# A two-layer encoder trunk: cosine product out of PSUM, first convolution steps on ScalarE, a pad of 32 bytes

## The chip, the cores and the metric

The kernel runs on one core of one Trainium2 chip. The metric is the device time of one execution in microseconds (us). The engines are TensorE (PE, matmuls into PSUM), VectorE (DVE), ScalarE (ACT), GpSimd (POOL) and SyncE (SP), whose queue here issues most DMA transfers. Each engine works through its own list of instructions in order; semaphores tie the lists together. PEclk in the profile is the granted clock of TensorE as a share of 2.4 GHz; 0.50 is 1.2 GHz.

## What is computed

Two sequences (1024 and 512 tokens, width 1024, fp32) go through two layers with shared weights and a last norm. Cut to the parts that the change and its neighbours touch:

```python
def apply_rope(x, cos, sin):                 # q and k of both attentions
    x1, x2 = jnp.split(x, 2, axis=-1)
    rot = jnp.concatenate([-x2, x1], axis=-1)
    return x * cos + rot * sin

def even_layer(h, ...):                      # layer 0
    u = h @ w_in
    glu, a_gate, q, k, v, b_gate = split_cols(u, EVEN_SPLITS)
    a_val, a_glu = jnp.split(glu, 2, axis=-1)
    a = a_val * jax.nn.sigmoid(a_glu)
    a = layernorm(depthwise_conv(a, conv_w, conv_b), ln_g, ln_b)      # 31 taps
    a = jax.nn.silu(a) * jax.nn.silu(a_gate)
    o = windowed_gqa(apply_rope(q), apply_rope(k), v, sink) * jax.nn.silu(b_gate)
    return jnp.concatenate([a, o], axis=-1) @ w_out

def odd_layer(h, ...):                       # layer 1
    q, k, v, c_gate, z, xbc, dt_f, dt_b = split_cols(h @ w_in, ODD_SPLITS)
    c = diff_attention(apply_rope(q), apply_rope(k), v, lam, diff_g) * jax.nn.silu(c_gate)
    xbc = jax.nn.silu(depthwise_conv(xbc, conv_w, conv_b))            # 5 taps
    d = mamba2_bidir(z, xbc, dt_f, dt_b, ...)                         # two chunked scans
    return jnp.concatenate([c, d], axis=-1) @ w_out
# x = x + layer(rmsnorm(x)) twice, then rmsnorm
```

## The kernel before

The 1536 tokens are three chunks of 512 (`g` = 0, 1 of the long sequence, 2 of the short one), channels lie on the 128 partitions. A projection tile is 128 output channels by 512 tokens: `proj` (L280 to L282) makes 24 matmuls of 128x512 into one PSUM accumulator, three for each of eight input blocks, since every fp32 operand is split into a high and a low half. The high half of a weight is a ScalarE copy (`wh`, L268), the low one a GpSimd subtraction (`wl`, L269).

The program runs in phases. A1: input norm, and of layer 0 the GLU projections, the 31-tap convolution (four units of 128 channels, each over all three chunks), the rotary k and q, some gates, and `conv_ln`, the layer norm over the convolved channels. A2: windowed attention and output projection. B1a: layer 1's dt and `xbc` projections with the 5-tap convolution, eight tiles of 128 channels. B1z: z and v. B1b: the scans, with layer 1's rotary k and q between them. B2: differential attention and output. O1: the last projection and norm.

What the change touches:

- `rope` (L374 to L385), 15 calls in A1 and 24 in B1b. ScalarE copies the accumulator into `r` (L378), four DMAs fetch the swapped halves into `rs` (L381), VectorE multiplies `r` by the cosines in place (L382), GpSimd multiplies `rs` by the sines (L383), VectorE adds (L384), a DMA writes the result. `r` and `rs` are two of four buffers of the tag `e2`, which the gates (L371, L372) and the tanh of the GLU (L428) share.
- `conv_units` (L433 to L471). When the three GLU products of a unit (L430, VectorE, one for each chunk, reading the value accumulator in PSUM) are there, `begin` sums neighbours into `xs` (L440) and starts three partial filters `fir` (L444, L446, L447); `taps` adds 15, 14 and 15 more products to them (L453, L456, L458), all in place on VectorE, 768 elements a partition each. `end` joins them (L464 to L466), and from the second unit on adds the unit to a sum (L471).
- `conv_ln` (L473 on): a mean matmul for each chunk (L479) into the tag `msx`, which has one bank in A1, four subtractions (L482) and squares, and then the scaling (L490, L491).
- `xbc` (L704 on): copies into `a` (L709), a first step on VectorE (L713), four taps (L716), Silu (L718).
- The PSUM accumulators of A1 rotate over five banks (`pj` and four `pjx`); in B1b nearly all use the one `pj`.

The order inside each engine's list is set when the program is built, by the framework's scheduler, which simulates a timeline and picks instructions that are ready; the source only gives priorities, by `merge` and `spread`, which lay projection units between convolution, scan and attention units. So an edit in one place can move instructions elsewhere.

## Time and profile before

| | us |
|---|---|
| median of three runs | 1711.17 (1710.85 to 1715.9) |
| profiled execution | 1710.5 |
| its span | 1708.7 |
| TensorE busy | 1586.7 (93%) |
| VectorE busy | 1132.5 (66%) |
| ScalarE busy | 708.1 (41%) |
| GpSimd busy | 677.5 (40%) |
| mean granted clock | 0.979 |

TensorE is busy nearly all the time, so the time follows its idle moments and its clock. They are found by stage: the table of stretches gives busy time and clock, the waits say what ended each idle moment, the groups by line give the duration of one instruction, and a timeline shows one place in order. A busy share of VectorE says little alone: what counts is where TensorE waits for it.

### The profile page before, as it was taken

What the parts mean: (1) busy time and instruction counts of PE and PEld (TensorE: products, weight loads), DVE (VectorE), ACT (ScalarE), POOL (GpSimd) and SP (SyncE); (2) the same over time, 40 slices, a digit from 0 to 9 for tenths busy, and PEclk for the clock granted to TensorE, in tenths of its full rate; (3) what the DMA queues carried; (4) which work ended last, traced back from release to release, by engine and by line L of the source; (5) the groups of instructions that cost most, each with busy time, mean ns of one, the idle gap of its engine ahead of it and who ended that gap; (6) DMA issues with size and microseconds to landing.
All of it is one profiled execution on the core that took longest, in us unless ns stands there. A gap on an engine that the chain in (4) does not pass through costs nothing.

```text
span 1708.7 us, 22696 instructions
## 1 busy us (share of the span) xinstructions
PE 1586.7 (93%) x7868; PEld 1303.6 (76%) x7868; DVE 1132.5 (66%) x1631; ACT 708.1 (41%) x1440; POOL 677.5 (40%) x531
## 2 busy tenths in 40 slices
PE   4998998889988989999999999989998999999997
PEld 3776787668777867867788887778877877888887
DVE  6788999954788786646664003796635677678554
ACT  6210111144676664433433112222225767668542
POOL 4244333333656545631311004654444534442340
PEclk9999999989999999999999999999999999999999
DMA  9011023335455447731433216664553545442562
GB/s 371 29 53 47 32 74 98 113 104 175 126 169 184 150 145 232 236 111 37 131 105 130 78 50 189 198 180 141 158 150 124 149 131 147 138 133 75 178 198 99
DMA packets 159109, 229.45 MB, mean 134 GB/s; under 512 B 18279, under 2 KB 70567, under 8 KB 158994
## 3 DMA queue, kind: packets, MB, share of 16 engines
q1 hardware_dynamic: 157074, 227.40, 42.2%
q8 instruction: 62, 1.02, 0.3%
q0 software_dynamic: 1920, 0.59, 0.2%
q14 instruction: 53, 0.43, 0.1%
HBM read 153.15 MB, written 64.55 MB: 127 GB/s over the span
## 4 chain that ended last, share of the span: by engine, by line
PE 30%; DMA 7%; DVE 4%; issue 4%; POOL 2%; SPq 2%; ACT 2%; POOLq 0%; DVEq 0%; ACTq 0%
PE ms L992 3%; PE pj L280 3%; PE pj L281 3%; PE pj L282 3%; DMA e<-e 2%; PE pjx L747 2%; PE pjx L746 2%; PE pjx L748 2%; PE s L967 2%; PE s L968 2%; PE pjx L280 1%; PE pjx L281 1%; PE pjx L282 1%; POOL e L383 1%; PE tr L390 1%
## 5 line engine op out<-in xcount | busy, mean ns | idle before, releaser
L269 POOL TENSOR_TENSOR wl<-wr,wh 128x512 fp32r<-128x512 f32 (+1 forms) x169 | 274.0, 1625 | 366.0 <-ACT wh L268 325.7
L282 PE MATMUL pjx<-x,wl 128*128 128x512 f32 (+1 forms) x712 | 286.4, 404 | 19.9 <-POOL wl L269 19.9
L280 PE MATMUL pjx<-x,wh 128*128 128x512 f32 (+1 forms) x712 | 287.4, 404 | 12.5 <-DVE e L372 8.0
L281 PE MATMUL pjx<-x,wh 128*128 128x512 f32 (+1 forms) x712 | 287.9, 405 | 6.3 <-DVE x L202 5.0
L280 PE MATMUL pj<-x,wh 128*128 128x512 f32 x604 | 247.4, 410 | 9.3 <-DVE e L372 5.0
L281 PE MATMUL pj<-x,wh 128*128 128x512 f32 x604 | 244.3, 404 | 3.9 <-DVE x L202 3.9
L282 PE MATMUL pj<-x,wl 128*128 128x512 f32 x604 | 241.9, 400 | 0.0
L268 ACT ACTIVATE wh<-wr 128x512 fp32r<-128x512 f32 (+1 forms) x169 | 105.5, 625 | 205.9 <-PE pjx L281 86.5
L282 PEld LDWEIGHTS pjx<-x,wl 128*128 128x128 f32 (+1 forms) x712 | 135.2, 190 | 55.5 <-POOL wl L269 23.0
L280 PEld LDWEIGHTS pjx<-x,wh 128*128 128x128 f32 (+1 forms) x712 | 134.8, 189 | 49.6 <-DVE e L372 10.4
L281 PEld LDWEIGHTS pjx<-x,wh 128*128 128x128 f32 (+1 forms) x712 | 134.8, 189 | 41.4 <-DVE x L202 6.6
L280 PEld LDWEIGHTS pj<-x,wh 128*128 128x128 f32 x604 | 115.6, 191 | 36.0 <-DVE e L372 6.1
L281 PEld LDWEIGHTS pj<-x,wh 128*128 128x128 f32 x604 | 115.3, 191 | 30.2 <-DVE x L202 5.1
L282 PEld LDWEIGHTS pj<-x,wl 128*128 128x128 f32 x604 | 115.3, 191 | 26.5 <-issue 0.2
L383 POOL TENSOR_TENSOR e<-e,cs 128x512 f32<-128x512 f32 x39 | 64.8, 1660 | 106.5 <-DMA e<-e 96.9
L976 ACT ACTIVATE pr<-s,nmx 128x1024 f32<-128x1024 f32 (+1 forms) x96 | 93.3, 975 | 27.6 <-DVE nmx L970 15.7
L177 POOL TENSOR_TENSOR r<-v,mhalf 128x4 f32<-128x4 f32 (+2 forms) x37 | 33.0, 892 | 140.5 <-DVE v L173 91.6
L992 PE MATMUL ms<-v,pT 128*128 128x128 f32 x640 | 81.2, 278 | 6.5 <-ACT pT L989 4.0
L992 PEld LDWEIGHTS ms<-v,pT 128*128 128x128 f32 x640 | 77.9, 193 | 10.6 <-ACT pT L989 4.4
L970 DVE TENSOR_REDUCE nmx<-s 128x1 f32<-128x1024 f32 x64 | 76.8, 1217 | 10.1 <-PE s L968 9.7
L517 POOL TENSOR_TENSOR raw<-raw,q 128x1024 fp32r<-128x1024 f32 x24 | 58.2, 2425 | 53.4 <-ACT q L515 49.0
L569 POOL TENSOR_SCALAR pr<-pr,den 128x384 f32<-128x384 f32 (+1 forms) x96 | 55.4, 597 | 50.0 <-DVE den L567 26.2
(360 smaller groups left out, 3393.1 us busy)
## 6 DMA issues: line engine op xcount, KB each, us to landing
wr<-in_wo SPq DMA_DIRECT2D x96, 256.0 KB, 3.7
wr<-in_w SPq DMA_DIRECT2D x87, 256.0 KB, 3.0
e<-e SPq DMA_DIRECT2D x156, 64.0 KB, 2.0
x<-xbd SPq DMA_DIRECT2D x22, 384.0 KB, 3.9
ct<-x1d SPq DMA_DIRECT2D x29, 256.0 KB, 3.6
raw<-q0d SPq DMA_DIRECT2D x48, 128.0 KB, 3.0
ct<-cat0d SPq DMA_DIRECT2D x24, 256.0 KB, 3.1
x1d<-e SPq DMA_DIRECT2D x24, 256.0 KB, 3.1
```

Of the source, the lines that this page charges most:

```text
L268: S.activation(out=wh, in_=raw, func=AF.Copy)
L269: G.tensor_tensor(out=wl, in0=raw, in1=wh.bitcast(F32), op=ALU.subtract)
L280: T_.matmul(acc, wh[:, kk, :], xh[:, k, :], start=(k == ks[0]), stop=False)
L281: T_.matmul(acc, wh[:, kk, :], xl[:, k, :], start=False, stop=False)
L282: T_.matmul(acc, wl[:, kk, :], xh[:, k, :], start=False, stop=(k == ks[-1]))
L383: G.tensor_tensor(out=rs, in0=rs, in1=cs_["sin"][:, cs], op=ALU.mult)
L517: G.tensor_tensor(out=lo, in0=raw, in1=q.bitcast(F32), op=ALU.subtract)
L569: G.tensor_scalar(out=prs[j], in0=prs[j], scalar1=den[:, j:j + 1], scalar2=1.0, op0=ALU.mult, op1=ALU.mult)
L746: T_.matmul(acc, xh[:, k, ts], hi[k], start=(k == 0), stop=False)
L970: V.tensor_reduce(out=nmx[:, t:t + 1], in_=o, axis=AX.XY, op=ALU.max, negate=True)
L976: S.activation(out=pr, in_=o if ncs > 1 else o[:, u:u + 1, :], func=AF.Exp, bias=nmx[:, u:u + 1], accum_out=den[:, u:u + 1])
L992: T_.matmul(oacc, pT[:, i, :], vtok[:, kt, :], start=(kt == 0), stop=(kt == NB - 1))
```

## The change

The cosine product of a rope is taken from the PSUM accumulator by VectorE, in a scalar_tensor_tensor into a third buffer `o`, and no longer from `r` after the copy; `r` is only read by the shuffles. The first step of each of the three partial filters, and that of `xbc`, is a ScalarE activation with scale and bias in place of VectorE's tensor_scalar: 12 and 8 instructions. The tag `e2` gets two further buffers in A1 and B1b (`e2x`), so that a rope takes three of six. A tile of 8 floats that nothing reads is allocated ahead of the others and set to zero. Lines move by 6 or 7: L382 becomes L386, L384 L391, L430 L437, L453 L459, L456 L462, L458 L464, L479 L485.

```diff
-    "A1": (dict(cs=2, a=2, xs=1, fir=3, y6=5), dict(pjx=4, msx=1)),
+    "A1": (dict(e2x=2, cs=2, a=2, xs=1, fir=3, y6=5), dict(pjx=4, msx=1)),
...
-    "B1b": (dict(rk=2, lk=4, cs=2, p4=4, x3=2, bc=2, ...
+    "B1b": (dict(e2x=2, rk=2, lk=4, cs=2, p4=4, x3=2, bc=2, ...
...
     def sb(tag, shape, dt=F32):
+        extra = ph["sb"].get(tag + "x", 0)
+        if extra:
+            n = ph["sb", tag] = (ph.get(("sb", tag), -1) + 1) % (SHARED[tag] + extra)
+            if n >= SHARED[tag]:
+                tag += "x"
         if tag in SHARED:
...
+    V.memset(tiny(8, "pad", 1), 0.0)
...
     def rope(acc, scale, g, dst):
         cs = pos(g)
-        r, rs = sb("e2", (P, CH)), sb("e2", (P, CH))
+        r, rs, o = (sb("e2", (P, CH)) for _ in range(3))
         S.activation(out=r, in_=acc, func=AF.Copy, scale=scale)
+        V.scalar_tensor_tensor(out=o, in0=acc, scalar=scale, in1=cs_["cos"][:, cs], op0=ALU.mult, op1=ALU.mult)
         for b in range(4):
-            o = b ^ 1
-            dma(out=rs[32 * b:32 * b + 32, :], in_=r[32 * o:32 * o + 32, :])
-        V.tensor_tensor(out=r, in0=r, in1=cs_["cos"][:, cs], op=ALU.mult)
+            f = b ^ 1
+            dma(out=rs[32 * b:32 * b + 32, :], in_=r[32 * f:32 * f + 32, :])
         G.tensor_tensor(out=rs, in0=rs, in1=cs_["sin"][:, cs], op=ALU.mult)
-        V.tensor_tensor(out=r, in0=r, in1=rs, op=ALU.add)
-        dma(out=dst[:, tok(g)], in_=r)
+        V.tensor_tensor(out=o, in0=o, in1=rs, op=ALU.add)
+        dma(out=dst[:, tok(g)], in_=o)
...
-            V.tensor_scalar(out=f[0], in0=a[:, :, 1:512:2], scalar1=cwh[:, j, 0:1],
-                            scalar2=prm[:, PC_CB + j:PC_CB + j + 1], op0=ALU.mult, op1=ALU.add)
-            V.tensor_scalar(out=f[1], in0=a[:, :, 0:513:2], scalar1=cwh[:, j, 1:2], scalar2=None, op0=ALU.mult)
-            V.tensor_scalar(out=f[2], in0=xs[:, :, 0:256], scalar1=cws[:, j, 0:1], scalar2=cb2[:, j:j + 1],
-                            op0=ALU.mult, op1=ALU.add)
+            S.activation(out=f[0], in_=a[:, :, 1:512:2], func=AF.Identity, scale=cwh[:, j, 0:1],
+                         bias=prm[:, PC_CB + j:PC_CB + j + 1])
+            S.activation(out=f[1], in_=a[:, :, 0:513:2], func=AF.Copy, scale=cwh[:, j, 1:2])
+            S.activation(out=f[2], in_=xs[:, :, 0:256], func=AF.Identity, scale=cws[:, j, 0:1], bias=cb2[:, j:j + 1])
...
-        V.tensor_scalar(out=acc, in0=a[:, :, 0:CH], scalar1=prm[:, wc:wc + 1],
-                        scalar2=prm[:, PC_SB + j:PC_SB + j + 1], op0=ALU.mult, op1=ALU.add)
+        S.activation(out=acc, in_=a[:, :, 0:CH], func=AF.Identity, scale=prm[:, wc:wc + 1],
+                     bias=prm[:, PC_SB + j:PC_SB + j + 1])
```

VectorE at the start of conv unit 0, before: the last GLU product (L430) of the unit, the neighbour sum (L440), the three first steps and the first taps (L345 and L346 belong to a constant).

```order
L430 SCALAR_TENSOR_TENSOR a_342<-e_58_453,pj_480 128x512
L345 TENSOR_TENSOR nlam<-ls 128x1
L440 TENSOR_TENSOR xs_594<-a_342 128x813
L346 TENSOR_SCALAR nlam<-nlam 128x1
L444 TENSOR_SCALAR fir_596<-a_342,cwh,prm 128x768
L446 TENSOR_SCALAR fir_597<-a_342,cwh 128x771
L447 TENSOR_SCALAR fir_598<-xs_594,cws,cb_318 128x768
L453 SCALAR_TENSOR_TENSOR fir_596<-a_342,cwh,fir_596 128x768
L456 SCALAR_TENSOR_TENSOR fir_597<-a_342,cwh,fir_597 128x771
L458 SCALAR_TENSOR_TENSOR fir_598<-xs_594,cws,fir_598 128x768
```

The same place after the change:

```order
L437 SCALAR_TENSOR_TENSOR a_347<-e_59_458,pj_485 128x512
L352 TENSOR_TENSOR nlam<-ls 128x1
L447 TENSOR_TENSOR xs_599<-a_347 128x813
L353 TENSOR_SCALAR nlam<-nlam 128x1
L459 SCALAR_TENSOR_TENSOR fir_601<-a_347,cwh,fir_601 128x768
L462 SCALAR_TENSOR_TENSOR fir_602<-a_347,cwh,fir_602 128x771
L459 SCALAR_TENSOR_TENSOR fir_601<-a_347,cwh,fir_601 128x768
L464 SCALAR_TENSOR_TENSOR fir_603<-xs_599,cws,fir_603 128x768
L462 SCALAR_TENSOR_TENSOR fir_602<-a_347,cwh,fir_602 128x771
L459 SCALAR_TENSOR_TENSOR fir_601<-a_347,cwh,fir_601 128x768
```

The three first steps are gone from VectorE's list, and taps follow the neighbour sum at once.

TensorE at `conv_ln`, before: the mean matmuls of the first two chunks (L479) stand in the last block of the gate accumulator `pjx_2404`, three matmuls apart.

```order
L280 MATMUL pjx_2404<-x_30_195,wh_2399 128x512
L479 MATMUL msx_2027<-y_150_1239,mean_w 128x512
L281 MATMUL pjx_2404<-x_31_196,wh_2399 128x512
L282 MATMUL pjx_2404<-x_30_195,wl_2400 128x512
L479 MATMUL msx_2065<-y_150_1239,mean_w 128x512
L280 MATMUL pjx_2487<-x_46_280,wh_2393 128x512
```

After the change the first stands in `pjx_2334`, an accumulator that ran two earlier, the second (below the dots, which leave out 29 rows) in the accumulator behind it:

```order
L288 MATMUL pjx_2334<-x_48_286,wh_2265 128x512
L289 MATMUL pjx_2334<-x_47_285,wl_2266 128x512
L485 MATMUL msx_2047<-y_154_1247,mean_w 128x512
L287 MATMUL pjx_2334<-x_47_285,wh_2265 128x512
...
L287 MATMUL pj_2454<-x_37_237,wh_2420 128x512
L485 MATMUL msx_2085<-y_154_1247,mean_w 128x512
L288 MATMUL pj_2454<-x_38_238,wh_2420 128x512
```

Counted from the start of the list, the first mean matmul moved from row 1205 to row 1141, and the three are 32 and 29 rows apart where they were 3 and 35.

VectorE in B1b, one rope among scan operations, before: its cosine product (L382) and its add (L384) follow each other.

```order
L865 TENSOR_TENSOR p_1741_9713<-p_1741_9713,p_1743_9722 128x1024
L890 TENSOR_TENSOR t_9746<-ms_9743,ed 128x512
L870 TENSOR_TENSOR p_1741_9713<-p_1741_9713,tr_9725 128x1024
L382 TENSOR_TENSOR e_1733_9655<-e_1733_9655,cs_8391 128x512
L384 TENSOR_TENSOR e_1733_9655<-e_1733_9655,e_1734_9656 128x512
L876 TENSOR_TENSOR y_9729<-y_9729,msx_9731 128x512
```

After the change a rope's product (L386) reads the accumulator `pj`, and two scan operations stand between it and its add (L391); the next rope's product follows.

```order
L386 SCALAR_TENSOR_TENSOR e2x_9528<-pj_9501,cs_8415 128x512
L871 TENSOR_TENSOR p_1730_9549<-p_1730_9549,p_1732_9558 128x1024
L876 TENSOR_TENSOR p_1730_9549<-p_1730_9549,tr_9561 128x1024
L391 TENSOR_TENSOR e2x_9528<-e2x_9528,e2x_9527 128x512
L386 SCALAR_TENSOR_TENSOR e_1753_9644<-pj_9617,cs_8415 128x512
L882 TENSOR_TENSOR y_9565<-y_9565,msx_9567 128x512
```

The product now stands where its accumulator is complete, ahead of the shuffles' end, and the add stays behind the sine product.

## Rows read from the trace of the kernel before

**Rows 1.** The page, first part: busy time, share of the span, instructions by engine.

```profile
PE 1586.7 (93%) x7868; PEld 1303.6 (76%) x7868; DVE 1132.5 (66%) x1631; ACT 708.1 (41%) x1440; POOL 677.5 (40%) x531
```

**Rows 2.** By stage: stretch, length, busy us (count) by engine, PEclk, DMA share, GB/s.

```profile
285.00:360.00 75.00, 59.48 (x234) 44.63 (x233) 66.39 (x71) 16.01 (x28) 21.72 (x14) 0.93 0.32 102
360.00:680.00 320.00, 294.11 (x1470) 241.37 (x1469) 228.70 (x474) 191.25 (x441) 168.64 (x171) 0.98 0.53 165
680.00:840.00 160.00, 159.04 (x725) 122.40 (x725) 97.93 (x137) 65.78 (x102) 64.22 (x44) 0.99 0.43 131
...
1030.00:1290.00 260.00, 244.68 (x1184) 200.97 (x1183) 163.19 (x199) 67.64 (x107) 135.10 (x129) 0.99 0.57 170
1290.00:1610.00 320.00, 303.74 (x1807) 261.63 (x1805) 226.48 (x338) 225.53 (x519) 126.98 (x81) 0.98 0.41 125
```

**Rows 3.** TensorE's waits, 285 to 360 us: us in total, times, longest us.

```profile
PE pjx L280 <- DVE e L372: 8.0, 3, 4.2
PE pjx L280 <- ACT wh L268: 2.2, 1, 2.2
PE msx L479 <- DVE y L482: 2.1, 1, 2.1
PE pjx L282 <- POOL wl L269: 2.1, 1, 2.1
PE pj L280 <- DVE e L372: 1.2, 1, 1.2
```

**Rows 4.** TensorE's waits, 66 to 200 us; timelines (start, us) of GpSimd and VectorE.

```profile
PE pjx L282 <- POOL wl L269: 13.8, 3, 6.4
...
166.18 1.29 POOL L269 TENSOR_TENSOR wl<-wr,wh 128x512 fp32r<-128x512 f32 x1 [7.76 <-ACT wh L268]
180.61 11.28 POOL L269 TENSOR_TENSOR wl<-wr,wh 128x512 fp32r<-128x512 f32 x2 [13.14 <-ACT wh L268]
...
185.04 1.01 DVE L458 SCALAR_TENSOR_TENSOR fir<-xs,cws,fir 128x768 f32<-128x768 f32 x1
...
217.52 0.69 DVE L430 SCALAR_TENSOR_TENSOR a<-e,pj 128x512 f32<-128x512 f32 x1 [6.23 <-PE pj L282]
```

**Rows 5.** By stage, columns as in group 2: the stretch at half clock.

```profile
347.90:358.10 10.20, 5.86 (x11) 3.55 (x12) 4.35 (x8) 5.37 (x9) 2.37 (x1) 0.50 0.32 103
```

**Rows 6.** VectorE by line, 224.1 to 345.5 us: count, busy us, mean ns, idle before.

```profile
L456 DVE SCALAR_TENSOR_TENSOR fir<-a,cwh,fir 128x771 f32<-128x771 f32 x22 | 27.9, 1267 | 0.0
...
L382 DVE TENSOR_TENSOR e<-e,cs 128x512 f32<-128x512 f32 x12 | 13.2, 1098 | 0.3 <-DMA e<-e 0.3
...
L372 DVE SCALAR_TENSOR_TENSOR e<-e,pjx 128x512 f32<-128x512 f32 x5 | 3.4, 673 | 0.0
...
L444 DVE TENSOR_SCALAR fir<-a,cwh,prm 128x768 f32<-128x768 f32 x1 | 1.1, 1068 | 0.0
```

**Rows 7.** ScalarE's waits, 224 to 346 us.

```profile
ACT e L378 <- DVE e L384: 38.1, 7, 10.1
```

**Rows 8.** Timelines: VectorE's sum for conv_ln, then TensorE at conv_ln.

```profile
341.03 1.76 DVE L471 TENSOR_TENSOR y<-y,y 128x1536 f32<-128x1536 f32 x1
...
339.19 0.50 PE L280 MATMUL pjx<-x,wh 128*128 128x512 f32 x1 [0.96 <-DVE e L372]
...
344.19 0.39 PE L280 MATMUL pjx<-x,wh 128*128 128x512 f32 x1
344.42 1.02 PE L479 MATMUL msx<-y,mean_w 128*128 128x512 f32 x2
```

**Rows 9.** ScalarE by line, whole span: columns as in group 6.

```profile
L718 ACT ACTIVATE y<-y 128x1536 f32<-128x1536 f32 x8 | 11.9, 1488 | 21.3 <-DVE y L716 21.3
```

**Rows 10.** VectorE's waits, 1030 to 1290 us; timeline of one rope there.

```profile
DVE e L382 <- DMA e<-e: 38.4, 16, 5.8
...
1183.03 0.58 ACT L378 ACTIVATE e<-pj 128x512 f32<-128x512 f32 x1
...
1185.32 0.47 PE L280 MATMUL pj<-x,wh 128*128 128x512 f32 x1
```

2 lines of the change are left out of this document (1 added, 1 removed).

## The prediction

> **What bounds the kernel now.** I read the page's first part first: TensorE is busy for 1586.7 of 1708.7 us, so all that any change can win is its 122 us of idle time and what a halved clock costs [rows 1]. The table by stage says where that lies. What the reader is to see in [rows 2]: from 680 to 840 us TensorE idles for 1 us only, so nothing can be won there; the stretch 285 to 360 us has 15.5 us of idle time and a mean granted clock of 0.93, with VectorE busy for 66.4 of 75 us. There VectorE is the bound. The waits of TensorE in that stretch name it [rows 3]: 8.0 + 1.2 us for gate products (L372) that stand in VectorE's queue between convolution taps, 2.1 us for conv_ln's subtraction, and 4.3 us for weights whose ScalarE copy or GpSimd half came late. From 347.9 to 358.1 us the granted clock is 0.50, the 1.2 GHz level, right after these idle moments; 10.2 us at half speed lose 5.1 us [rows 5]. So about 15.6 + 5.1 = 20.7 us is the most that the stretch can give.
>
> Earlier in A1 (66 to 200 us) TensorE waits three times, 13.8 us in all, for the low half of a weight from GpSimd [rows 4]. Here two GpSimd subtractions in a row, with their inputs there, last 11.28 us together, while a single one lasts 1.29 us, and VectorE runs taps of 1.01 us without a gap, of which one row stands. GpSimd is held up for as long as that run of taps lasts.
>
> **The change part by part.** The profiled execution took 1710.5 us (span 1708.7, 1.8 outside it), 0.7 us below the median of 1711.17; I sum against 1710.5.
>
> *Conv steps, units 0 to 2.* Each unit's three first steps (1.07 us each, [rows 6]) leave VectorE. But the order of VectorE shows three more taps in their place before the next GLU product, which waits for TensorE anyway (6.23 us in the last of these waits, [rows 4]): 25, 33 and 36 taps stood there before, 28, 36 and 40 now. VectorE is given the same amount of work in front of the same wait, so the first two stalls for GpSimd stay: 0. At the third (beside the 11.28 us) the new ScalarE steps start only behind a tanh that ScalarE makes for the gate, so VectorE may have a gap in which GpSimd is let in. That can win between 0 and a third of the 13.8 us, 4.6; I take 2, nearer to nothing, since at the other two the taps close up.
>
> *From the last GLU product to conv_ln (224 to 343 us), VectorE.* Three things go. The first steps of unit 3: 3 x 1.07 = 3.2 us. Nine taps that are done earlier now (69 stood behind the last GLU product, 60 now): 9 x 1.27 = 11.4 us at the mean of this window [rows 6], 9 x 1.01 = 9.1 us at that of an undisturbed tap [rows 4]. And 12 cosine products of 1.098 us become products with an input in PSUM; the nearest row is L372, the same operation and shape out of PSUM, 0.673 us [rows 6]: 12 x 0.425 = 5.1 us, or 0, if a product that took long because GpSimd worked beside it only passes that on to a tap. The bounds are so 3.2 + 9.1 = 12.3 and 3.2 + 11.4 + 5.1 = 19.7 us; I take 15, the lower half, since GpSimd's products stay. VectorE ended this work at 341.03 + 1.76 = 342.8 us [rows 8]; now at about 328.
>
> *The same stretch, TensorE.* conv_ln's first mean matmul started at 344.4 us [rows 8]; in the new order it stands 64 matmuls further forward (the second fence of the section on the change), which at 0.23 us from start to start is 14.7 us. Before, TensorE passed that point at 344.4 - 14.7 - 2.2 = 327.5 us (2.2 us are the two gate waits in between, 1.2 and 0.96). Without the waits in front of it (2.2 + 2.1 for weights and 9.2 - 4.2 - 2.2 = 2.8 for a gate) it would be there at 320.4. But it can't pass before VectorE's 328: 0.5 us later than before, after a wait of some 7 us. What it lost behind that point was 2.2 + 2.1 + 4.2 us of waits and 5.1 us of clock, 13.6 us in all [rows 3, 5]. The three mean matmuls are some 30 matmuls (7 us) apart now instead of 3 matmuls, so the wait for their single bank should go, and the gate products should be done early, since VectorE is ahead. After the new wait of 7 us the clock may fall again as it did at 347.9 us. Gain 13.6 - 0.5 = 13.1 without a fall, 8.0 with all of it; with VectorE's 12.3 (2.7 us later) and a fall 5, with 19.7 and none 17.8. I take 10.
>
> *ScalarE in A1.* Its rope copies wait for the buffers that VectorE's add frees: 38.1 us over seven copies, up to 10.1, and weight copies queue behind them [rows 7]. Three buffers of six in place of two of four keep two ropes in flight as before; but the add comes sooner, since the product no longer waits for the shuffle. This is where the 2.2 + 2.1 us for weights in [rows 3] should go; they stand ahead of conv_ln's point and only bring TensorE to the wait there sooner, so I count nothing more. Twelve conv steps of 768 elements are added to ScalarE, between 0.58 us (512 elements, [rows 10]) and 1.49 us (1536, [rows 9]), about 1 us each, on an engine that is busy for 16 of 75 us [rows 2]: 0.
>
> *xbc steps (B1a).* Eight steps of 1536 elements leave VectorE, and eight of some 1.5 us (L718's, of the same shape) go to ScalarE [rows 9], with one more load of a function table (ten where nine stood). TensorE idles for 1 us of 160 there [rows 2], and ScalarE is busy for 66: nothing to win, up to 2 to lose where the copy that frees an accumulator queues behind a step; 0.5.
>
> What VectorE's steps are worth can be weighed otherwise. The row gives 1.07 us for 768 elements [rows 6], no faster than a tap. The Trainium skill ("VectorE: DVE Perf Modes", the perf-mode tier table) lets an fp32 tensor-scalar operation on SBUF operands run at two elements a cycle. By it the three steps of unit 3 would be worth about half, and the sum some 1.5 us less; the trace does not show that form in these steps, and the measured durations decide.
>
> *Ropes in B1b.* VectorE's 38.4 us of waiting for the shuffles move from the product to the add, where they are paid as well [rows 10]; TensorE does not see them. The new price is the bank: nearly all of these accumulators use one bank, which is free again only when the ScalarE copy and then the product have read it. In the shown rope the copy runs from 1183.03 to 1183.61 and the next accumulator starts at 1185.32, 1.7 us later [rows 10]. The product adds 0.67 us (L372's duration), and what VectorE has in hand at that moment, of the order of 1 us. That fits in the 1.7 us mostly. VectorE saves up to 24 x 0.425 = 10 us; if TensorE's 15.3 us of idle time [rows 2] shrink by a fifth, the gain is 3, and by a fifth of rival 2's price the loss is 5; taken +0.5.
>
> *A2, B2 and the pad.* No operation changes there, but the order does: gate matmuls that fill waits stand elsewhere. TensorE idles for 25.9 us in A2 and 16.3 us in B2 [rows 2]; a fifth of that either way is 5 us, taken 0. The pad moves later tiles by 32 bytes and adds one memset of 8 columns: operations on tiles at either offset last alike (0.673 us for L372, 0.69 for L430, [rows 4, 6]), so 0.
>
> Sum: -2 - 10 + 0.5 + 0.5 = -11; 1710.5 - 11 = 1699.5, against the median 1700.
>
> **Rivals.** *(1) The gain is eaten at conv_ln.* TensorE arrives early at the mean matmul that was put forward, waits the full 7 us, and its clock falls for as long as at 347.9 us, VectorE having won its lower bound; GpSimd's third stall stays. For it: the freed time of VectorE was filled with taps before, and the mean matmul has 15 us less work in front of it. Against: the matmuls in front of it do not vanish, they run behind it. It gives 5 from that stretch and nothing from the third stall: 1710.5 - 5 + 1 = 1706.5, and up to 1713 where the new order of A2 and B2 takes 5 more.
>
> *(2) The bank in B1b.* Each of the 24 accumulators is held until VectorE comes to the product: 0.67 us and on average half an operation of 1.1 us, 1.2 us, x 24 = 29 us on TensorE. Then 1710.5 - 12 + 0.5 + 29 = 1728. It decides where VectorE is more than about 1 us behind when the copy ends (1.7 us of room less the product's 0.67). Against it: VectorE is busy for 163 of 260 us, and TensorE has score and state matmuls between the ropes. Half of the price would bring the time to 1713.5, two thirds to 1718. The Trainium skill ("PSUM — Partial Sum Buffer", the section on bank collisions) says that two engines must not read one bank at once, ScalarE and VectorE among them; the new order agrees, the product is behind the copy, and no run so far shows its price.
>
> *(3) More than counted.* The third stall goes whole (4.6) and the clock stays up at conv_ln with VectorE's full 19.7 us (17.8): 1710.5 - 22.4 + 1 = 1689, or 1686 with the 3 us of B1b.
>
> *(4) The change doesn't do what it says.* If the product out of PSUM cost as much as it saves (1.1 us, say, since it may hold GpSimd's sine product up too), VectorE's saving is 12.3 us and the gain at conv_ln 5: 1710.5 - 7 + 1 = 1704.5, at the edge of rival 1's reach, and counted with it.
>
> **How the numbers follow.** Forecast 1700, chance 0.58, its own range 1692 to 1706; rivals 1 and 4 0.22 (1704.5 to 1713); rival 2 0.14 (1714 to 1728); rival 3 0.06 (1686 to 1690). A measurement of this kernel can tell about 0.3% (5 us) from no change, so faster means under 1706 and slower over 1716. Faster: 0.56 of the forecast's 0.58 and rival 3, 0.62; the same: 0.02 + 0.22 = 0.24; slower: rival 2, 0.14. The range from 1686 to 1714 leaves out rival 2 and some 0.03 at each end.
>
> **What would show it.** Right: VectorE reaches conv_ln's sum some 15 us sooner than 342.8 us; TensorE's waits for L372 in 285 to 360 us fall from 9.2 to under 3 us and its idle time there from 15.5 to under 8 us; the product out of PSUM lasts 0.67 to 0.69 us; the two early waits for GpSimd stay at about 10 us. Wrong: a wait of over 5 us at the first mean matmul with a granted clock of 0.50 behind it (rival 1); TensorE's idle time from 1030 to 1290 us up from 15 to 30 us or more, released by the product (rival 2); A2's or B2's stretch longer by more than 5 us, which I count as noise of the new order.

## The result, and the profile after

The changed kernel takes 1684.07 us (median of four runs, 1680.1 to 1687.51) where the kernel before takes 1711.01: 0.9838 of it, with a 95% interval of 0.9807 to 0.9870. That is 27 us. The forecast was 11 us and the range ended at 1686, so the sign was right and the size wrong.

The profiled execution took 1680.1 us, the shortest of the four, with a span of 1678.3. The page's first part, as in [rows 1] for before:

```profile
PE 1572.0 (94%) x7868; PEld 1304.9 (78%) x7868; DVE 1088.0 (65%) x1612; ACT 734.1 (44%) x1461; POOL 661.7 (39%) x531
```

TensorE's idle time fell from 122 to 106.3 us, its busy time from 1586.7 to 1572.0. The matmuls are the same, and the mean granted clock is no higher (0.979 before, 0.977 after), so the second difference is not time at the lower clock; the section on the pad shows where it comes from. VectorE is busy for 44.5 us less. The two stretches by stage that hold A1's end (columns as in [rows 2]):

```profile
200.00:285.00 85.00, 77.54 (x325) 63.17 (x324) 79.17 (x79) 15.36 (x24) 37.81 (x18) 0.94 0.28 84
285.00:360.00 75.00, 68.52 (x309) 55.62 (x309) 62.53 (x76) 26.12 (x43) 28.52 (x19) 0.98 0.32 101
```

From 285 to 360 us TensorE idles for 6.5 us where it idled for 15.5 [rows 2], and the granted clock is 0.98 in place of 0.93; but the stretch before it, which had no idle time and a granted clock of 1.00, has 7.5 us and 0.94 now. TensorE's waits from 200 to 362 us say what these are (us in total, times, longest us):

```profile
PE msx L485 <- DVE y L477: 5.4, 1, 5.4
PE pj L289 <- POOL wl L276: 4.4, 1, 4.4
PE pjx L289 <- POOL wl L276: 3.1, 1, 3.1
PE pjx L287 <- DVE e L379: 1.1, 1, 1.1
```

The waits for a gate product, 9.2 us before [rows 3], are down to 1.1 us. Two new ones for the low half of a weight (7.5 us) and one at `conv_ln`'s first mean matmul (5.4 us) have come. Earlier, from 66 to 200 us, two of the three old waits for GpSimd still stand, 12.3 us where they were 10.4:

```profile
PE pjx L289 <- POOL wl L276: 12.3, 2, 7.5
```

VectorE's sum for `conv_ln` (now L477), and TensorE there; start, us:

```profile
323.00 1.76 DVE L477 TENSOR_TENSOR y<-y,y 128x1536 f32<-128x1536 f32 x1
```

```profile
324.81 2.07 PE L485 MATMUL msx<-y,mean_w 128*128 128x512 f32 x2 [5.36 <-DVE y L477]
...
327.11 0.63 PE L288 MATMUL pjx<-x,wh 128*128 128x512 f32 x1
327.54 0.63 PE L289 MATMUL pjx<-x,wl 128*128 128x512 f32 x1
```

VectorE ends the sum at 324.8 us; it was 342.8 [rows 8]. TensorE came to the mean matmul at 324.81 - 5.36 = 319.5 us and waited. The matmuls behind it are 0.43 us apart where they were 0.23 apart ahead of the wait: this is the lower clock, and the mean granted clock from 324.9 to 335 us is 0.84.

To compare kernels whose parts begin at different times I cut every profiled execution at three places that all of them have, each read from a timeline: the end of the last score matmul of A2 (L553 before), the end of the first scan matmul of B1b (L859), the end of the last rope's ScalarE copy (L378), and the end of ScalarE's last operation. In us:

| kernel | start to last A2 score | to first scan matmul | B1b, to last rope copy | to the end |
|---|---|---|---|---|
| before | 624.3 | 412.5 | 236.1 | 426.7 |
| after | 608.3 | 412.3 | 232.0 | 417.0 |
| e1 conv, rope in A1 | 612.9 | 415.6 | 239.7 | 426.0 |
| e2 conv | 620.2 | 414.4 | 238.5 | 423.5 |
| e3 rope in A1 | 616.6 | 413.7 | 238.2 | 425.5 |
| e4 rope in B1b | 626.1 | 414.2 | 231.3 | 440.1 |
| e5 rope | 616.6 | 411.6 | 231.4 | 417.3 |
| e6 xbc | 624.1 | 412.8 | 236.9 | 423.5 |
| e7 after, no pad | 611.1 | 413.3 | 232.5 | 420.2 |
| e8 after, old rope in B1b, no pad | 615.2 | 414.0 | 236.7 | 421.3 |
| e9 after, ring from 0 | 607.7 | 408.9 | 231.6 | 430.5 |
| e10 after, ring from 2 | 610.6 | 409.9 | 230.5 | 422.5 |
| e11 rope in B1b, ring from 3 | 624.7 | 413.7 | 234.0 | 420.2 |
| e12 after, ring from 4 | 611.2 | 412.4 | 232.0 | 415.8 |
| e13 ring in B1b | 625.5 | 413.5 | 238.8 | 423.0 |
| e14 after, four buffers | 611.7 | 410.2 | 229.4 | 421.0 |
| e15 pad | 624.5 | 409.7 | 235.5 | 428.0 |
| e16 after, weights on VectorE | 585.9 | 406.2 | 232.0 | 418.8 |
| e17 pad of 64 bytes | 624.7 | 411.8 | 237.4 | 424.5 |
| e18 after, weights and sines on VectorE | 581.2 | 412.7 | 231.3 | 416.9 |

Each row is one execution. Kernels that do the same in the same order on TensorE scatter by 2 us in the first column (before, e4, e6, e11, e13, e15 and e17: 624.1 to 626.1), but by more in the last: 421.0 to 428.0 where B2 and O1 have the order of before, and 430.5 and 440.1 in e9 and e4, which also share one order. So a single difference of a few us says nothing, but groups do.

### The profile page after: what moved, and what is told of

It reads as the page before. It is cut to its first block, busy times and chain, and to the rows that moved or that the text cites. A ratio compares the mean times of both kernels' runs of the same rounds, so it can differ in the third digit from the quotient of the medians.

```text
span 1678.3 us, 22679 instructions
## 1 busy us (share of the span) xinstructions
PE 1572.0 (94%) x7868; PEld 1304.9 (78%) x7868; DVE 1088.0 (65%) x1612; ACT 734.1 (44%) x1461; POOL 661.7 (39%) x531
## 4 chain that ended last, share of the span: by engine, by line
PE 35%; DMA 6%; DVE 3%; issue 3%; ACT 2%; SPq 1%; POOL 1%; POOLq 0%; DVEq 0%; ACTq 0%
PE pj L287 4%; PE pj L288 4%; PE pj L289 4%; PE ms L998 3%; PE pjx L752 2%; PE pjx L754 2%; PE pjx L753 2%; PE s L973 1%; PE s L974 1%; PE pjx L288 1%; PE pjx L289 1%; PE pjx L287 1%; PE tr L397 1%; PE trx L397 1%; DMA raw<-k1d 1%
## 5 line engine op out<-in xcount | busy, mean ns | idle before, releaser
L276 POOL TENSOR_TENSOR wl<-wr,wh 128x512 fp32r<-128x512 f32 (+1 forms) x169 | 270.3, 1604 | 346.8 <-ACT wh L275 335.7
L289 PE MATMUL pjx<-x,wl 128*128 128x512 f32 (+1 forms) x712 | 281.3, 398 | 16.4 <-POOL wl L276 16.4
L288 PE MATMUL pjx<-x,wh 128*128 128x512 f32 (+1 forms) x712 | 284.1, 399 | 6.6 <-DVE x L209 5.2
L287 PE MATMUL pjx<-x,wh 128*128 128x512 f32 (+1 forms) x712 | 284.4, 400 | 5.0 <-ACT wh L275 3.3
L722 DVE SCALAR_TENSOR_TENSOR y<-a,prm,y 128x1536 f32<-128x1536 f32 x32 | 59.1, 1848 | 20.6 <-ACT y L719 20.1
```

Of the source, the lines that this page charges most:

```text
L276: G.tensor_tensor(out=wl, in0=raw, in1=wh.bitcast(F32), op=ALU.subtract)
L287: T_.matmul(acc, wh[:, kk, :], xh[:, k, :], start=(k == ks[0]), stop=False)
L288: T_.matmul(acc, wh[:, kk, :], xl[:, k, :], start=False, stop=False)
L289: T_.matmul(acc, wl[:, kk, :], xh[:, k, :], start=False, stop=(k == ks[-1]))
L722: V.scalar_tensor_tensor(out=acc, in0=a[:, :, t:t + CH], scalar=prm[:, wc + t:wc + t + 1], in1=acc, op0=ALU.mult, op1=ALU.add)
```

## The experiments

Each "Measured" line gives the median of a run, the median of the kernel before on the same chip, and their ratio with its 95% interval.

### Which part holds the gain (e1 to e8)

The first question was where the 16 us lie that the forecast had not counted. In e2 only the conv steps change:

```diff
-            V.tensor_scalar(out=f[0], in0=a[:, :, 1:512:2], ...)      # and f[1], f[2]
+            S.activation(out=f[0], in_=a[:, :, 1:512:2], ...)         # and f[1], f[2]
```

> The kernel before with only the twelve conv steps on ScalarE. If VectorE's time up to conv_ln sets A1, the three first steps of unit 3 and the nine taps done earlier count (12 to 15 us of VectorE) and the gain is most of that of A1: 1699 to 1703. If ScalarE's rope copies, which wait for the add's buffer, set it, the conv steps are worth little: 1706 to 1711.

Measured: 1707.2 against 1712.4, 0.9965 (0.9943 to 0.9988). VectorE's sum for `conv_ln` ends 106.2 us after the last GLU product, where it took 118.7 before: 12.5 us, as the first theory has it. But less than half of it stays (4 us in the first column, 5 to 6 by the runs). TensorE waits more for weights, 9.2 us from 200 to 375 us, and ScalarE's rope copies still wait for the add's buffer, for longer than in [rows 7] (ScalarE's waits, 224 to 340 us):

```profile
ACT e L378 <- DVE e L384: 49.5, 8, 9.7
```

In e3 only the rope of A1 changes, with its two buffers:

```diff
-    "A1": (dict(cs=2, ...
+    "A1": (dict(e2x=2, cs=2, ...
...
     def rope(acc, scale, g, dst):
+        if "e2x" not in ph["sb"]:
+            return rope_old(acc, scale, g, dst)
```

> The kernel before with only the new rope and its two buffers in A1; TensorE's order is that of the kernel before but for six rows. If VectorE's time up to conv_ln sets A1: 12 products shorter by 0.4 us, up to 5 us of VectorE, 1706 to 1709. If ScalarE's copies waiting for the add's buffer set it, most of A1's gain is here: 1696 to 1702.

Measured: 1704.9 against 1712.4, 0.9948 (0.9932 to 0.9964), between the two theories' ranges, though with almost the order of before. VectorE does not come sooner: 119.5 us from the last GLU product to the sum, 0.8 more than before. Its lines from 225.9 to 348 us (columns as in [rows 6]; L472, L475, L477 are the taps, L398 the product, L403 the add):

```profile
L472 DVE SCALAR_TENSOR_TENSOR fir<-a,cwh,fir 128x768 f32<-128x768 f32 x23 | 31.5, 1370 | 0.0
L477 DVE SCALAR_TENSOR_TENSOR fir<-xs,cws,fir 128x768 f32<-128x768 f32 x24 | 29.8, 1242 | 0.0
L475 DVE SCALAR_TENSOR_TENSOR fir<-a,cwh,fir 128x771 f32<-128x771 f32 x22 | 24.8, 1128 | 0.0
L403 DVE TENSOR_TENSOR e2x<-e2x,e2x 128x512 f32<-128x512 f32 x6 | 8.5, 1412 | 1.2 <-POOL e2x L402 1.2
L403 DVE TENSOR_TENSOR e<-e,e 128x512 f32<-128x512 f32 x6 | 4.1, 679 | 0.0
...
L398 DVE SCALAR_TENSOR_TENSOR e<-pjx,cs 128x512 f32<-128x512 f32 x5 | 3.4, 680 | 0.0
```

The rows of before that go with them and that [rows 6] does not show:

```profile
L458 DVE SCALAR_TENSOR_TENSOR fir<-xs,cws,fir 128x768 f32<-128x768 f32 x24 | 31.4, 1309 | 0.0
...
L453 DVE SCALAR_TENSOR_TENSOR fir<-a,cwh,fir 128x768 f32<-128x768 f32 x23 | 27.3, 1188 | 0.0
...
L384 DVE TENSOR_TENSOR e<-e,e 128x512 f32<-128x512 f32 x12 | 9.2, 770 | 0.0
```

The product lasts 0.680 us, as forecast, 0.42 less than in [rows 6]. But the twelve adds take 12.6 us where they took 9.2, since six of them now run beside a GpSimd operation and last 1.41 us on the mean, and the neighbour sum and the joins of the filters take 2 us more. The taps do not change: one line rises from 1.19 to 1.37 us, the two others fall, and all three together take 86.1 us where they took 86.6. What the product no longer loses to GpSimd, other operations lose, the adds above all. So the lower bound of the forecast's term, nothing, was right. What the rope brings in A1 is not VectorE's time. ScalarE's copies no longer wait for the add, the two waits for weights in [rows 3] are gone, and TensorE's waits from 285 to 362 us halve:

```profile
PE pj L285 <- DVE e L377: 4.7, 1, 4.7
PE msx L498 <- DVE y L501: 2.1, 1, 2.1
PE pjx L285 <- DVE e L377: 0.9, 1, 0.9
```

In the changed kernel the 38 us of rope copies waiting for the add are gone too; from 221 to 330 us ScalarE waits longest for TensorE, and for an add it waits once, 5.8 us with a gate's tanh.

In e1 both stand together, and in e4 the rope of B1b alone:

```diff
# e1: the conv steps of e2 and the rope of e3
# e4, with the two ropes of e3:
-    "B1b": (dict(rk=2, ...
+    "B1b": (dict(e2x=2, rk=2, ...
```

> The kernel before with the twelve conv steps on ScalarE and the new rope (with its two buffers) in A1 only; xbc, B1b and the pad as before. Up to xbc its order is that of the changed kernel. Theory 1 (all of the gain is made in A1, where VectorE reaches conv_ln sooner, and the rest of 30 us is chance of the order): 1681 to 1686, as the changed kernel. Theory 2 (A1 gives what its own stretch shows, 16 us up to the first score of A2, and another 11 us are made by the ropes in B1b): 1693 to 1697, VectorE's sum for conv_ln ends at 325 us as in the changed kernel.

Measured: 1703.1 against 1712.4, 0.9937 (0.9916 to 0.9958), so 10.8 us: neither theory's number. What A1 gives in its own stretch (11 to 14 us in the first column) is nearly all that e1 keeps; theory 1 is out, and theory 2's 16 us were too many.

> The kernel before with only the new rope and its two buffers in B1b; everything ahead of B1b in the same order as before. Theory 1: within 3 us of before, 1708 to 1714. Theory 2: 1698 to 1703, with the first score matmul of B2 some 10 us sooner. The rival of the prediction (the bank held for copy and product) would give over 1716.

Measured: 1717.3 against 1712.4, 1.0023 (1.0003 to 1.0043). By the number this is the rival's, but the bank is not its cause: B1b itself is 5 us shorter (231.3), and the last column 13 us longer. The two theories are out by the number. So the rope of B1b has two effects, and the second one needs its own test.

e5 takes the rope in both phases, e6 only xbc, e7 and e8 take one thing off the changed kernel:

```diff
# e5: rope as in the change, e2x=2 in A1 and B1b; no conv, no xbc, no pad
# e6:
-        V.tensor_scalar(out=acc, in0=a[:, :, 0:CH], ...)
+        S.activation(out=acc, in_=a[:, :, 0:CH], ...)
# e7: the changed kernel without
-    V.memset(tiny(8, "pad", 1), 0.0)
# e8: the changed kernel without the pad, with e2x=2 and the new rope in A1 only
```

> The kernel before with the new rope and its buffers in A1 and B1b, nothing else. Its order up to B1b is that of the kernel with the rope in A1 only (1705), in B1b and B2 that of the changed kernel. Theory A (the 17 us that A1 does not explain come from the ropes of B1b and the order of B2 that goes with them): 1688 to 1693. Theory B (they come from xbc on ScalarE): 1703 to 1708. Theory C (from the pad): 1703 to 1708.

Measured: 1691.7 against 1711.4, 0.9896 (0.9856 to 0.9936): theory A.

> The kernel before with only the eight xbc steps on ScalarE. A1, B1z, B1b and B2 keep their order on TensorE. The prediction's account: TensorE idles for 1 us there, so 1710 to 1713. Theory A and C: the same. Theory B: 1694 to 1698.

Measured: 1710.4 against 1711.4, 0.9990 (0.9972 to 1.0008): nothing, as forecast; theory B is out.

> The changed kernel without its pad; the order is the same on every engine, only tiles lie 32 bytes lower. Prediction, theories A and B: no difference, 1682 to 1687. Theory C: 1695 or more.

Measured: 1688.1 against 1711.4, 0.9868 (0.9837 to 0.9900), just over the expected 1687. Its interval and that of the changed kernel overlap, so the 4 us between them are not clear of noise by themselves; the pad comes back below.

> The changed kernel with the old rope and four buffers in B1b and without the pad: B1b and B2 in the order of the kernel before, all ahead of them in that of the changed kernel. Theory A: 1700 to 1704. Theory B: 1683 to 1687. Theory C: 1700 to 1704.

Measured: 1699.3 against 1711.4, 0.9934 (0.9911 to 0.9956), just under theory A's range. It lacks 15 to 16 us of the changed kernel's gain and 11 of e7's, which ran on the same chip and has no pad either. What it lacks against e7 is B1b's rope and the order of B2 that goes with it.

### B1b: the product ahead of the shuffles, or the larger ring (e13, e14)

The third column of the table has two groups without overlap: 229.4 to 234.0 us in the eleven kernels with the new rope in B1b, 235.5 to 239.7 in the nine with the old one; the means differ by 5.9 us. e13 has only the larger ring there, e14 only the product:

```diff
# e13: the kernel before, with
+    "B1b": (dict(e2x=2, rk=2, ...
# e14: the changed kernel, with e2x=2 struck out in A1 and B1b
```

> The kernel before with only the two further buffers in B1b (old rope, two of six). TensorE's order is that of the kernel before up to the end of B1b, B2 gets another one. Theory product (B1b's 6 us come from the product that no longer waits for the shuffles ahead of scan operations on VectorE): 236 to 240 us from the first scan matmul to the last rope's copy, as in the six runs with the old rope. Theory buffers (they come from the larger ring): 230 to 234 us.

Measured: 1712.4 against 1714.3, 0.9992 (0.9977 to 1.0008), and 238.8 us in B1b.

> The changed kernel without the further buffers: a rope takes three of four, so the next one waits for a buffer. B1b: theory product 230 to 235 us, theory buffers 236 us or more. In A1 ScalarE's copies wait for a buffer again as before the change (38 us in the kernel before, 0 in the changed one), and TensorE's waits for weights behind them come back: the whole 3 to 12 us over the changed kernel, 1687 to 1696, if B2's order, which is the kernel before's, gives nothing.

Measured: 1681.8 against 1714.3, 0.9798 (0.9773 to 0.9823), and 229.4 us in B1b. So it is the product. The two buffers are worth nothing: the rope with four buffers is as fast as with six. The half of the expectation on A1 was wrong: ScalarE does wait for buffers again (224 to 330 us; a buffer comes free with the DMA that writes the result), and the time does not suffer from it, in an order that differs much in A1:

```profile
ACT e L385 <- DMA q0d<-e: 45.4, 8, 11.2
```

How the product helps is in VectorE's and TensorE's waits. First B1b as a whole, before and after (columns as in [rows 2]):

```profile
1036.70:1272.90 236.20, 224.41 (x1104) 185.51 (x1102) 159.29 (x194) 63.15 (x100) 124.35 (x122) 0.99 0.55 165
```

```profile
1020.60:1252.50 231.90, 224.49 (x1110) 188.65 (x1110) 145.40 (x194) 64.16 (x102) 116.00 (x124) 0.98 0.57 171
```

TensorE's idle time there falls from 11.8 to 7.4 us, VectorE's work from 159.3 to 145.4. This holds for every profile: between the same two places TensorE idles for 9.5 to 11.8 us in the nine kernels with the old rope and for 5.3 to 8.0 in the eleven with the new one.

VectorE's waits for the rope before are 38.4 us for the shuffles [rows 10] and, behind them, for the sine product

```profile
DVE e L384 <- POOL e L383: 16.9, 14, 2.2
```

55 us together. After, the add waits for the sine product, and the product waits for ScalarE's copy, which reads the accumulator ahead of it (VectorE's waits, 1014 to 1257 us):

```profile
DVE e2x L386 <- ACT e L385: 65.1, 3, 62.7
DVE e L391 <- POOL e L390: 16.3, 8, 5.0
DVE e L386 <- ACT e L385: 14.3, 5, 5.3
DVE e2x L391 <- POOL e2x L390: 13.5, 7, 4.5
```

The wait of 62.7 us is the start of the phase, where VectorE waited for 64.0 us before as well, with another operation. Without it these are 46.5 us. In e13, with the old rope, the waits for the shuffles are there (1039 to 1279 us):

```profile
DVE e L387 <- DMA e<-e: 15.4, 8, 5.7
...
DVE e2x L387 <- DMA e2x<-e2x: 9.4, 6, 3.8
```

All of e13's waits for the rope are 46.6 us, no more than after the change, and its B1b is not shorter than before. So the time that VectorE waits is not what decides; what stands behind the wait is. VectorE's list runs in order, and TensorE waits for scan operations in it: `y` (L876), `p` (L870), `nx` (L834). TensorE's longest waits in B1b before:

```profile
PE msx L875 <- DVE p L870: 2.5, 1, 2.5
...
PE msx L875 <- DVE y L876: 1.8, 1, 1.8
...
PE ms L887 <- DVE nx L834: 1.6, 1, 1.6
```

and after, where the lines are L882, L876 and L840:

```profile
PE msx L881 <- DVE p L876: 4.3, 1, 4.3
...
PE pj L287 <- DVE e2x L386: 0.7, 1, 0.7
```

By the timeline of before, this `y` and a further `nx` (0.6 us) stand behind a product that had waited 4.4 us for its shuffles, and the `nx` of 1.6 us behind a product of 1.66 us and an add of 1.52 us. These three waits, 4.0 us, are gone after the change. The waits for `p` have no rope operation just ahead of them, and they stay. Whether it is the product's earlier place or VectorE's 14 us less of work that takes the three away, no run separates.

The bank, the prediction's rival, costs TensorE one wait of 0.7 us for a product (`pj` behind L386).

### The order of B2 (e9 to e12)

e4 and e5 have the same rope in B1b, and their last columns are 23 us apart. What differs is which of the six buffers a rope of B1b gets: the rotation goes on from A1 in e5 and starts in B1b in e4, and the scheduler, which sees other buffers come free at other times, lays B2 out in another way. So I set the start of the rotation by hand, with nothing else changed:

```diff
     phase("B1b")
+    ph["sb", "e2"] = -1          # e9: buffer 0 first; e10: = 1, buffer 2; e12: = 3, buffer 4; e11: = 2, buffer 3, in the kernel of e4
```

> The changed kernel, but the rotation over the six e2 buffers starts at its first buffer in B1b (in the changed kernel it comes there at its fourth). No instruction is added or removed, TensorE's order is the same up to B1b, in B2 it becomes that of the kernel with the new rope in B1b only (1717). Theory A1 (B2's order is worth what the traces show, 21 us between these two orders, whatever the ropes cost): 1702 to 1710. Theory A2 (the ropes themselves make the gain, the order of B2 is worth under 5 us): 1683 to 1689.

Measured: 1695.1 against 1712.9, 0.9880 (0.9852 to 0.9908).

> The changed kernel with the rotation started at its third buffer in B1b; B2 gets the order of the kernel before. Theory A1: B1b keeps its 5 us, B2 loses the 6 us that the changed kernel's order gave: 1689 to 1695. Theory A2: 1683 to 1689.

Measured: 1683.6, 0.9815 (0.9789 to 0.9841).

> The kernel before with the new rope in B1b only, as in the run that gave 1717, but with the rotation started at its fourth buffer, so that B1b and B2 get the changed kernel's order; all ahead is as before. Theory A1: 5 us from B1b and 6 us from B2: 1698 to 1704. Theory A2, by the run that gave 1717: 1712 to 1720.

Measured: 1701.2, 0.9911 (0.9880 to 0.9942). This is e4 with another buffer first, and 16 us less.

> The changed kernel with the rotation started at its fifth buffer in B1b; B1b in the changed kernel's order, B2 in an order that no run so far has. Theory A1: B1b as in the changed kernel (232 us from the first scan matmul to the last rope's copy), B2 anything from 6 us less to 15 us more than before's order: 1680 to 1706. Theory A2: 1683 to 1689.

Measured: 1681.9, 0.9808 (0.9784 to 0.9831).

So the order of B2 counts, since theory A2 fails for e9 and e11; but theory A1 fails for e9 and e10, and the order is worth less than single profiles had suggested: 11 to 13 us between e9 and the others, and the order of the kernel before (e10) is no worse than the changed kernel's. By the last column the changed kernel's order gains 5 to 6 us over that of before (416.9 to 420.2 in six kernels against a mean of 424.2 of the ten kernels with the latter, 421.0 to 428.0); by the runs of e10 against the changed kernel, nothing. That part stays open. What is worse in the order that e4 and e9 share can be read. The stretch from the last rope's copy to the last score matmul of B2, before, after, e4, e9:

```profile
1272.90:1592.00 319.10, 302.06 (x1752) 258.16 (x1753) 222.97 (x333) 220.84 (x503) 128.58 (x81) 0.98 0.42 129
```

```profile
1252.50:1561.20 308.70, 296.56 (x1744) 252.68 (x1742) 221.40 (x330) 220.57 (x500) 124.43 (x79) 0.99 0.43 131
```

```profile
1271.60:1605.80 334.20, 310.23 (x1743) 261.35 (x1741) 232.55 (x331) 220.62 (x504) 126.80 (x80) 0.96 0.40 121
```

```profile
1248.20:1572.50 324.30, 301.78 (x1743) 255.58 (x1741) 231.34 (x331) 220.18 (x504) 129.02 (x80) 0.98 0.41 124
```

e4 and e9 need 334 and 324 us for what takes 309 to 319 us in the others, and VectorE's time in operations is some 9 us longer in both. The 10 us between them are not TensorE's order, which is the same in both from there on: the execution of e4 that was profiled is the longest of its ten (1722.2 us), that of e9 the shortest of its four. TensorE's waits for the softmax's exponential in e4 and in the changed kernel:

```profile
PE s L986 <- ACT pr L995: 10.3, 14, 1.9
```

```profile
PE s L973 <- ACT pr L982: 4.6, 6, 1.4
```

In e4 score matmuls wait 14 times for the exponential (ScalarE, `pr`) and lose 10.3 us, in e9 15 times and 10.1 us; six waits of 4.6 us in the changed kernel. That other units stand where these moments would have to be filled is the likely reason; it is not shown.

### The pad (e15, e17)

```diff
# e15: the kernel before, with
+    V.memset(tiny(8, "pad", 1), 0.0)
# e17: the same with tiny(16, ...)
```

> The kernel before with only the pad: every instruction in the same order, later tiles 32 bytes higher. No mechanism in the traces: no difference, 1709 to 1713. If the pad is worth what the changed kernel and its copy without pad differ by (0.9838 and 0.9868 of before), 1706.

Measured: 1707.0 against 1714.3, 0.9951 (0.9933 to 0.9968). All six of its runs (1705.46 to 1708.69) are below all seventeen of the kernel before on that chip (1709.47 to 1719.81), in an order that is the same on every engine.

> The kernel before with a pad of 64 bytes in place of 32: every instruction in the same order, and every later tile at the same place within 64 bytes as before the change. If the pad of 32 bytes helps by where tiles begin within 64 bytes: as the kernel before, 0.998 to 1.002 of it. If any shift does it, or the extra instruction: 0.993 to 0.997, as the pad of 32 bytes alone (0.9951).

Measured: 1710.4 against 1712.1, 0.9987 (0.9970 to 1.0004). That is in the range of no effect, and its interval begins just above the end of e15's, on another chip. So neither any shift nor the extra instruction seems to do it, but the place within 64 bytes at which tiles begin, and the profiles bear that out.

Operations of VectorE, ScalarE and GpSimd last alike: for every line with four or more of them the tenth percentile of the durations agrees within 0.005 us between the profiles of before and e15. TensorE's do not. From 200 to 285 us it never idles and its granted clock is 1.00 in before, e15 and e17, which have the same order there (columns as in [rows 2]):

```profile
200.00:285.00 85.00, 85.00 (x366) 68.44 (x365) 78.46 (x78) 11.87 (x20) 31.79 (x18) 1.00 0.25 75
```

```profile
200.00:285.00 85.00, 84.99 (x375) 70.12 (x374) 79.36 (x78) 11.86 (x20) 32.41 (x18) 1.00 0.25 75
```

```profile
200.00:285.00 85.00, 85.00 (x366) 68.28 (x365) 77.58 (x77) 11.87 (x20) 30.16 (x18) 1.00 0.25 74
```

In the same 85 us TensorE runs 375 matmuls with the pad of 32 bytes and 366 without it or with 64. Over the whole profiles the median from start to start of two projection matmuls of 128x512, with no idle time and not at half clock, is 227 ns in all eight kernels with the pad of 32 bytes and 233 or 234 ns in the twelve others. On the mean this is 4.5 ns less in e15 than before, over some 3800 such matmuls 17 us. The time falls by 7 us only. Part of the rest goes back at the lower clock: the mean granted clock of e15's six runs is 0.972, that of the seventeen of before on that chip 0.975, which is some 5 us. Why the place of a tile sets the pace of the matmuls, and why the clock gives part of it back, is not shown.

### What is left in A1 (e16, e18)

The waits for GpSimd that remain in A1 (12.3 + 4.4 + 3.1 us) are low halves of weights. GpSimd's operations there, start and us, and the three of the first row by themselves (shortest, median and longest, ns):

```profile
141.32 15.64 POOL L276 TENSOR_TENSOR wl<-wr,wh 128x512 fp32r<-128x512 f32 x3 [10.77 <-ACT wh L275]
164.05 1.30 POOL L276 TENSOR_TENSOR wl<-wr,wh 128x512 fp32r<-128x512 f32 x1 [7.09 <-ACT wh L275]
```

```profile
L276 POOL TENSOR_TENSOR wl<-wr,wh x3: 1268/1271/13172, 141.3 to 155.7; 128x512 fp32r<-128x512 f32 x3
```

One alone takes 1.30 us. Of the three in a row the first takes 13.17 us and ends at 154.5 us, the others take 1.27 each. VectorE runs taps without a gap until 153.4 us and then waits for TensorE (start, us):

```profile
152.35 1.01 DVE L462 SCALAR_TENSOR_TENSOR fir<-a,cwh,fir 128x771 f32<-128x771 f32 x1
158.51 0.69 DVE L437 SCALAR_TENSOR_TENSOR a<-e,pjx 128x512 f32<-128x512 f32 x1 [5.14 <-PE pjx L289]
```

So the subtraction is held until VectorE runs out of taps. The prediction had this as a matter that the change leaves as it is. But e3 showed that the time which GpSimd and VectorE take from each other does not vanish when one of them is spared it, and that suggests the way out: let VectorE do this work itself.

```diff
-            G.tensor_tensor(out=wl, in0=raw, in1=wh.bitcast(F32), op=ALU.subtract)
+            ph.get("wl", G).tensor_tensor(out=wl, in0=raw, in1=wh.bitcast(F32), op=ALU.subtract)
...
     run(gl[0][1])
     load_cs()
+    ph["wl"] = V
...
+    ph["wl"] = G
     conv_ln()
```

> The changed kernel, with the low halves of the weights from the second conv unit to the last rope of A1 subtracted on VectorE and not on GpSimd. Theory (a GpSimd operation beside taps costs VectorE as much time as it takes itself, so that its work is free for VectorE to take over): VectorE's time from the last GLU product to conv_ln stays within 5 us of 103, TensorE's four waits for weights (20 us with 7 us of half clock) shrink to under 8 us: 1668 to 1677. Rival (each subtraction adds its 0.9 us to VectorE, 23 of them, and delays the taps): conv_ln 15 to 20 us later, 1688 to 1700.

Measured: 1655.2 against 1714.3, 0.9652 (0.9629 to 0.9674): 59 us faster than the kernel before, some 30 more than the change. That beats even the theory's number, and one of its sentences is wrong: from the last GLU product to `conv_ln` VectorE takes 117.8 us, not 103, because the GLU products come 22 us sooner and leave more taps behind them, 72 in place of 60. TensorE's waits for low halves from 66 to 330 us, which were 19.8 us:

```profile
PE pjx L289 <- POOL wl L276: 1.0, 1, 1.0
PE pj L289 <- POOL wl L276: 0.3, 1, 0.3
```

VectorE's new subtraction, 66 to 330 us:

```profile
L276 DVE TENSOR_TENSOR wl<-wr,wh 128x512 fp32r<-128x512 f32 x22 | 15.0, 683 | 4.4 <-ACT wh L275 4.4
```

22 subtractions cost VectorE 15.0 us. The three lines of taps give back 5.4 us (199.9 to 194.5) and the adds 2.8 us: about half is conserved, not all. The rest of the gain is a circle that opens. VectorE's waits in the changed kernel (66 to 325 us) and in e16 (66 to 317 us):

```profile
DVE a L437 <- PE pjx L289: 10.4, 2, 5.3
DVE a L437 <- PE pj L289: 5.8, 1, 5.8
```

```profile
DVE a L437 <- PE pjx L289: 0.2, 1, 0.2
```

VectorE waited 16.2 us for the GLU accumulators of TensorE, which waited for weights from GpSimd, which VectorE's taps held up until it had none left.

e18 moves A1's sine products to VectorE as well:

```diff
-        G.tensor_tensor(out=rs, in0=rs, in1=cs_["sin"][:, cs], op=ALU.mult)
+        ph.get("wl", G).tensor_tensor(out=rs, in0=rs, in1=cs_["sin"][:, cs], op=ALU.mult)
```

> The changed kernel with weights' low halves and also the sine products of A1's ropes on VectorE, so that GpSimd does next to nothing beside the taps. Theory (GpSimd's time beside taps costs VectorE as much): fifteen products of 0.68 us on VectorE against fewer taps of 2 us, conv_ln within 4 us of the kernel with only the weights moved, and adds that no longer wait: 1651 to 1658. Rival (VectorE is the bound by then and only gets the work on top): 1660 to 1668.

Measured: 1650.7 against 1712.1, 0.9633 (0.9607 to 0.9659), as the theory has it. Its interval overlaps e16's, so that the sine products are worth anything on top is not shown; the two are the fastest kernels here.

## Why the prediction was wrong

**A1, VectorE: right.** The term was 15 us with bounds of 12.3 and 19.7. From the last GLU product to `conv_ln`'s sum it is 15.3 us (118.7 to 103.4). Its parts were not as put: the conv steps alone give 12.5 us (e2), near the lower bound of 3.2 + 9.1, and the product nothing (e3), the term's lower end: the product's lost time passes on, to the adds above all. That VectorE comes sooner is not by itself the gain, though: in e14, in another order, it ends the sum at 313.1 us, 11.6 sooner than in the changed kernel, and the first column is no shorter (611.7 against 608.3).

**A1, TensorE: nearly right.** The wait at the mean matmul is 5.4 us (some 7 forecast), the bank's wait of 2.1 us is gone, the gate waits are 1.1 us (under 3), and the clock did fall after the wait. With the third wait for GpSimd the forecast was 12 us; the first column of the table gives 11.9 us on the mean of the three kernels with both edits and without the pad (e1, e7 and e8 against before, e4, e6, e11 and e13), and the runs of e1, which has only A1's part, 10.8. With the pad it is another 3.6 us (after, e9, e10 and e12). In e7 TensorE's waits from 66 to 362 us are 21.1 us in place of 29.4; in the changed kernel they are 26.3, probably because its matmuls run faster and come to the waits sooner. The step on unit 2's third wait failed: it was to win 2 us, but it only moved, to 206.6 us, and a fourth came at 273.2 us.

**ScalarE in A1: mis-sized.** "I count nothing more" for the waits of copies and weights was wrong for the rope alone: e3 wins 7.5 us, with VectorE no sooner at `conv_ln`. Whether the copies' 38.1 us are the cause stays open, since in e14 they wait 45.4 us again and the first column hardly suffers from it.

**B1a: right.** xbc is worth nothing (e6).

**Ropes in B1b: this step failed.** It said that VectorE's waits for the shuffles "move from the product to the add, where they are paid as well; TensorE does not see them". The first half was near the truth: 55 us of waits for the rope became 46.5, now for the copy and the sine product. The second half failed: TensorE saw them, through the scan operations queued behind on VectorE, and its idle time in B1b fell by more than a third (11.8 to 7.4 us) where the forecast had a fifth at best. The term was a loss of 0.5 us, between a gain of 3 and a loss of 5; it measures a gain of 5.9 (eleven kernels with the new rope against nine with the old one). The rival of the held bank has one wait of 0.7 us. The rule of the Trainium skill that stood beside it ("PSUM — Partial Sum Buffer", the section on bank collisions) only sets the order of the two readers, and here that order was cheap: VectorE's products wait 16.7 us for the copies, and TensorE hardly waits for the products; by the row of 1183.03 to 1185.32 us in [rows 10] there was room.

**A2, B2: mis-sized.** "A fifth either way", 5 us, was too narrow for the order: a change of B2's order alone moves the time by 13 us (e9 against e12) and by 16 us (e4 against e11). In the changed kernel it gives between 0 and 5 us of gain.

**The pad: this step failed.** It was put at nothing because operations last alike at either offset, by two rows of VectorE. VectorE's do; the projection matmuls do not, they start every 227 ns in place of 233. The pad alone measures 7 us on one chip (e15), and with the rest of the change some 4 (e7, not clear of noise). Why the offset sets the pace is open.

In sum, A1 11 to 12 us of gain (12 forecast), B1b 6 (a loss of 0.5 forecast), order of B2 0 to 5, pad 4 to 7 (both 0 forecast): 21 to 30 us, with the 27 measured between. So the sign of the forecast rests on A1, which it had right, and the missing 16 us on three terms that it had put at about nothing.

## What to carry to other kernels

A wait inside an engine that works in order is paid by whatever is queued behind it: when an instruction is moved ahead of a DMA's end, look not only at its own chain and at the sum of the waits but at who waits for the instructions that stood behind it. When tiles move in memory, compare the pace of every engine that reads them, TensorE's too. Where a scheduler sets the order, a term for "the order changes" needs bounds from real orders; here a mere change of the first buffer in a ring was worth 13 us. And where a long run of VectorE work and GpSimd's work on SBUF overlap, ask first whether the bound engine could do GpSimd's part itself: it cost 15 us of VectorE's time and saved some 30.
